# Making half of the second query tile from x * g behind the first products, and keeping two first tiles and this one in SBUF

## The chip, the cores and the metric

The kernel runs on one core of one Trainium2 chip, as one launch. The metric is device microseconds of one execution. The kernel before takes 1150.07 us, the median of three runs (1149.07 to 1150.61).

## What is computed

One layer of a decoder trunk on a sequence of 1024 tokens and 1024 channels, in float32. The part that matters here is its start: a normalised and modulated input u, and one combined projection of it.

```python
def _rmsnorm(x, g):
    y = x32 * lax.rsqrt(jnp.mean(x32 * x32, axis=-1, keepdims=True) + EPS)
    return y.astype(x.dtype) * g

u = _rmsnorm(h, g_mix) * (1 + scale1) + shift1          # scale1, shift1 from silu(c) @ W_ada + b_ada
proj = u @ w_in                                          # [q | k | v | us | gate_att | gate_ssm]
...                                                      # dilated attention, S5 branch, merge, w_out
h = h + gate1 * merged @ w_out
h = h + gate2 * ConvGatedMLP(modulate(h))
out = rmsnorm(h, g_final)
```

q, k and v have 512 columns each (8 heads of 64), us has 256, and each gate has 1024.

## The kernel before

**Precision.** Every product of two float32 matrices is made of three matmuls in a fast float32 form. Each operand is split into a high part (ScalarE, a copy) and a low part (VectorE, the value less its high part), and `mm3` (L188) adds high x high, high x low and low x high in one PSUM bank. A product of a 128-column weight tile with 512 tokens over 1024 channels is thus 8 x 3 = 24 matmuls of 128 x 512.

**Start.** Channels lie on the partitions, tokens along the free axis, and "half" 0 or 1 is the first or last 512 tokens. For each of eight channel tiles k, x is loaded (`load_x`, L330), and its 128 modulation factors g = g_mix * (1 + scale1) come from row dots of W_ada with silu(c) on VectorE (`row_dot`, L326). `xg[k]` is x * g, split in high and low. The products with weights `w0` (first 128 columns of q, first 128 of k, all 256 of us: four tiles) start from xg at once (loop at L424 to L453): x * g needs no token norm, since 1/rms is one factor for each token and can be put on afterwards, and the shift adds a constant per output column. Seven of the eight (tile, half) pairs are made there, each in its own PSUM bank, in the order of `b0` (L341): (1,0), (2,0) in banks of tag "s", (0,0), (3,0) in "t", (1,1), (2,1) in "mm", (0,1) in "o". The eighth, (3,1), is made much later from u (`gen_us`, L649). There are eight PSUM banks, two of each tag.

**The token norm.** The same x is loaded a second time with tokens on the partitions (`xn`, L352). ScalarE squares and sums each of eight tiles (L356), then `root` (L394) makes 1/rms: a table load and one activation (L397), one square (L399), two short VectorE corrections (L400, L401). `spread_a` (L405) puts it on the diagonal of four 128 x 128 blocks on ScalarE (L408), and `spread_b` (L410) multiplies by a matrix of -1 on TensorE (L413) and copies the bank to `rr` (L414). The list `late` (L416) says at which place of the product loop each of these is emitted.

**After it.** With rr known, `u_half` (L478) makes u for one channel tile and one half: VectorE (L1482), ScalarE (L1483), VectorE (L1488). `scale_r` (L466) multiplies a bank of first products by rr into `t0`, a tile in SBUF, which gives the bank back. The constant of each output column comes from a product of the weights with the shift (L494, L495: sixteen matmuls of 512 columns), transposed in `bias_cols` (L507). Then v is made for all tokens (L573 to L614): half 0 of u with banks s, s, t, t, then half 1 with mm, mm, o, o, 192 matmuls in all, while VectorE and ScalarE make the next u tiles between them; `put_q`, `put_k`, `put_v` and `put_us` write results out in split form.

**Attention.** `attention` (L1575) goes in steps of score, softmax, transpose and product with v, starting `LEAD` = 9 steps early. Between them it takes "fill" units from `gen_fill` (L659): one unit is one `mm3`. The fills make the q and k tiles of the head pairs 1 to 3 from u (`gen_qk`, L638: four groups of eight units each), the eighth us half, and then the gates and projections. Their pace is a count wanted per step: `FILL_PACE` = 1.55 units until 96 have been made, then `SLOW_PACE` = 1.52 (L1685 to L1689). Each engine runs its instructions in the written order; the pace uses a clock of its own (`unit`), not the chip's.

**Loads.** All loads of this part are issued by SyncE, in order; a weight tile uses one of two single staging buffers, "wvx" for even and "wraw" for odd numbers (`load_w`, L299).

## Time and profile before

| what | value |
|---|---|
| three timed executions | 1150.07, 1150.61, 1149.07 us |
| the profiled execution | 1151.31 us |
| its span, first to last instruction | 1149.2 us |
| mean granted TensorE clock | 0.990 of full |
| HBM read, written | 126.20 MB, 31.46 MB |

All times inside the program below are microseconds from the start of the span. The profile gives for each instruction its engine (PE is TensorE's matmul, DVE VectorE, ACT ScalarE, POOL GpSimd, SPq the load queue of SyncE), the line of the kernel, the tile written and read, and in brackets the idle time before it with the instruction that ended this wait. Matmuls overlap in the array, so the time from start to start, and not the duration shown, is what one costs in a row of them. A granted clock of 0.50 means that the array ran at half speed.

### The profile page before, as it was taken

To read this page: it belongs to the slowest core of one execution; us is meant where nothing else is said; L and a number is where in the kernel's file an instruction comes from. 1 tells how busy PE (TensorE), PEld (TensorE's weight loads), DVE (VectorE), ACT (ScalarE), POOL (GpSimd) and SP (SyncE) were. 2 spreads that over 40 slices of the span, in tenths; PEclk is the share of its full clock that TensorE was granted. 3 is DMA by queue.
4 is the path that set the end of the run, shared out by engine and by line. 5 is a ranking of instruction groups with operands and counts; after the bars stand their busy time and mean duration, and the time that the engine had idled before them with its cause. 6 is when DMAs were issued, how large, how long until landed. Compare 5 with 4: busy or idle time off the path is not lost.

```text
span 1149.2 us, 14743 instructions
## 1 busy us (share of the span) xinstructions
PE 1110.8 (97%) x5286; PEld 914.6 (80%) x5286; DVE 863.8 (75%) x1656; ACT 582.8 (51%) x1065; POOL 150.6 (13%) x171
## 2 busy tenths in 40 slices
PE   9899999999999999989899999999999999999995
PEld 8677888888878888878788887788888888877784
DVE  6678687876569598168786779888877768879876
ACT  3648777778832313243234565452445336726653
POOL 1001444445422212100000000000000000000003
PEclk9999999999999999989999999999999999999998
DMA  9811111111022221235583352245424337779433
GB/s 366 351 55 57 63 38 38 48 45 65 11 76 81 49 84 55 74 123 180 185 352 121 96 234 74 92 174 193 140 80 144 113 110 264 251 260 376 149 128 147
DMA packets 57338, 159.20 MB, mean 139 GB/s; under 512 B 7441, under 2 KB 13713, under 8 KB 55473
## 3 DMA queue, kind: packets, MB, share of 16 engines
q1 hardware_dynamic: 47520, 144.56, 35.2%
q10 hardware_dynamic: 9744, 13.70, 3.8%
q8 instruction: 41, 0.67, 0.2%
q14 instruction: 33, 0.26, 0.1%
HBM read 126.20 MB, written 31.46 MB: 137 GB/s over the span
## 4 chain that ended last, share of the span: by engine, by line
PE 63%; DVE 13%; DMA 8%; issue 8%; ACT 7%; POOL 1%; SPq 0%; POOLq 0%; ACTq 0%; DVEq 0%
PE ps_s L1335 10%; PE ps_mm L1335 8%; PE ps_mm L190 7%; PE ps_mm L192 7%; PE ps_mm L191 7%; PE ps_t L1335 7%; PE ps_s L190 3%; PE ps_s L192 3%; PE ps_s L191 3%; DMA xn<-in_xn 2%; PE ps_t L1643 2%; PE ps_s L1607 1%; PE ps_o L1660 1%; PE ps_s L1608 1%; DVE op L892 1%
## 5 line engine op out<-in xcount | busy, mean ns | idle before, releaser
L1335 PE MATMUL ps_s<-op,half 128*128 128x512 f32 x792 | 190.0, 390 | 5.2 <-ACT ps_s L1349 3.2
L1335 PEld LDWEIGHTS ps_s<-op,half 128*128 128x128 f32 x792 | 148.0, 188 | 38.7 <-ACT ps_s L1349 4.5
L190 PE MATMUL ps_mm<-u,whl 128*128 128x512 f32 x360 | 144.1, 400 | 1.6 <-DVE V L534 1.1
L192 PE MATMUL ps_mm<-u,whl 128*128 128x512 f32 x360 | 140.8, 391 | 0.0
L191 PE MATMUL ps_mm<-u,whl 128*128 128x512 f32 x360 | 140.5, 390 | 0.0
L1335 PE MATMUL ps_mm<-op,half 128*128 128x512 f32 x528 | 125.2, 389 | 0.0
L1335 PEld LDWEIGHTS ps_mm<-op,half 128*128 128x128 f32 x528 | 99.1, 188 | 20.6
L1335 PE MATMUL ps_t<-op,half 128*128 128x512 f32 x432 | 103.9, 389 | 0.7 <-ACT tp L1343 0.7
L1335 PEld LDWEIGHTS ps_t<-op,half 128*128 128x128 f32 x432 | 81.0, 188 | 17.9 <-ACT tp L1343 1.1
L121 POOL TENSOR_TENSOR whl<-wraw,whl 128x256 fp32r<-128x256 f32 (+2 forms) x52 | 63.4, 1220 | 203.1 <-ACT whl L118 203.1
L1449 POOL TENSOR_TENSOR hh<-hh,acc 128x512 f32<-128x512 f32 x3 | 4.3, 1441 | 654.3 <-ACT acc L1438 654.3
L192 PEld LDWEIGHTS ps_mm<-u,whl 128*128 128x128 f32 x360 | 67.6, 188 | 14.8
L190 PEld LDWEIGHTS ps_mm<-u,whl 128*128 128x128 f32 x360 | 67.8, 188 | 13.6 <-issue 2.2
L191 PEld LDWEIGHTS ps_mm<-u,whl 128*128 128x128 f32 x360 | 67.8, 188 | 10.4
L1648 DVE TENSOR_TENSOR PT<-ps_t,PT 128x512 fp32r<-128x512 f32 (+1 forms) x80 | 50.6, 633 | 28.2 <-ACT PT L1646 27.7
L1141 DVE TENSOR_TENSOR half<-scr,half 128x512 fp32r<-128x512 f32 x80 | 54.5, 685 | 16.2 <-ACT half L1140 15.9
L118 ACT ACTIVATE whl<-wraw 128x256 fp32r<-128x256 f32 (+2 forms) x72 | 48.7, 676 | 28.3 <-PE ps_s L192 14.6
L1619 ACT ACTIVATE S<-S,mcol 128x128 f32<-128x128 f32 (+3 forms) x64 | 49.3, 771 | 14.5 <-DVE mcol L1617 12.9
L1623 POOL TENSOR_SCALAR S<-S,mcol 128x128 f32<-128x128 f32 (+3 forms) x64 | 48.5, 761 | 50.0 <-DVE mcol L1622 29.2
L1140 ACT ACTIVATE half<-scr 128x512 fp32r<-128x512 f32 x80 | 49.0, 626 | 8.8 <-DVE scr L1122 6.7
L1141 DVE TENSOR_TENSOR half<-wraw,half 128x512 fp32r<-128x512 f32 x66 | 45.1, 686 | 8.0 <-ACT half L1140 7.9
L1646 ACT ACTIVATE PT<-ps_t 128x512 fp32r<-128x512 f32 (+1 forms) x80 | 43.7, 550 | 10.4 <-PE ps_t L1643 9.3
(516 smaller groups left out, 2430.9 us busy)
## 6 DMA issues: line engine op xcount, KB each, us to landing
wraw<-in_wup SPq DMA_DIRECT2D x32, 512.0 KB, 3.6
fq<-f SPq DMA_DIRECT2D x16, 1024.0 KB, 5.3
ft<-fq SPq DMA_DIRECT2D x14, 1024.0 KB, 7.8
ada<-in_wada SPq DMA_DIRECT2D x24, 512.0 KB, 8.8
wraw<-in_wdn SPq DMA_DIRECT2D x20, 512.0 KB, 5.7
adaB<-in_wada ACTq DMA_DIRECT2D x16, 512.0 KB, 4.3
wraw<-in_wout SPq DMA_DIRECT2D x16, 512.0 KB, 3.6
hd<-h SPq DMA_DIRECT2D x12, 512.0 KB, 7.5
```

The lines of the kernel that those rows point to most:

```text
L118: nc.scalar.activation(w[:, 0, cs], raw[:, cs], AF.Copy)
L121: lo.tensor_sub(w[:, 1, cs], raw[:, cs], w[:, 0, cs].bitcast(F32))
L190: nc.tensor.matmul(ps, wh, xh, start=first, stop=False)
L191: nc.tensor.matmul(ps, wh, xl, start=False, stop=False)
L192: nc.tensor.matmul(ps, wl, xh, start=False, stop=last)
L1140: nc.scalar.activation(w[:, 0], src, AF.Copy)
L1141: lows.append(lambda: nc.vector.tensor_sub(w[:, 1], src, w[:, 0].bitcast(F32)))
L1335: mm = lambda wp, xp, i: nc.tensor.matmul(ps, w[:, wp, ws], xp[:, cs], start=first and k + i == 0, stop=k == KT // 2 - 1 and i == 2, skip_ ...
L1619: nc.scalar.activation(tl, tl, AF.Exp, bias=mc[:, 0:1], scale=-1.0, accum_out=mc[:, 2:3])
L1623: nc.gpsimd.tensor_scalar(tl, tl, mc[:, 3:4], 0.0, op0=OP.mult, op1=OP.add)
L1646: nc.scalar.activation(pt[:, 0, :w], tps[:, :w], AF.Copy)
L1648: 0, lambda: nc.vector.tensor_sub(pt[:, 1, :w], tps[:, :w], pt[:, 0, :w].bitcast(F32)))
```

## The change

- A ninth weight tile of the start, number 8, holds the second 128 columns of q (`wq[1]`). Its load is issued in the loop at k = 4, its high part is made at k = 6 and its low part at (7, 0), ahead of `root`. It uses the staging buffer "wvx", which weight 4 (the first of v) uses after it.
- At k = 7 the first two finished banks, (1,0) and (2,0), are copied by ScalarE to their `t0` tiles in SBUF (`keep`). Their norm factor is put on later, from SBUF to SBUF.
- One of the two "s" banks so freed takes a new product, half 0 of the second q tile from xg: a loop of eight `mm3` behind the first products. `spread_b(0)` is emitted inside this loop, ahead of its seventh `mm3` (`SPREAD_AT` = 6). The product is called (3, 1) in `t0`.
- Its column constant needs sixteen matmuls of 128 columns more and a copy `brow1`, which is emitted ahead of the second `u_half`.
- `scale_r` works on (3,1) in the place of (1,0) in the first `u_half`; (1,0) and (2,0) come at k = 2 and k = 5 of the v loop.
- In attention, `gen_qk` makes only three groups for head pair 1; the finished half `q1` is written by `put_q`. The pace of the fills is 1.42 until 88 units (`FILL_QK`).

The diff, cut to its core (line numbers of the order below differ by one from the kernel before up to L413, since one line is added at the top):

```diff
+SPREAD_AT, FILL_QK = 6, 88
-LEAD, FILL_PACE, SCORE_PACE = 9, 1.55, 1.2
+LEAD, FILL_PACE, SCORE_PACE = 9, 1.42, 1.2
-            src = I["w0"][i] if i < 4 else I["wv"][i - 4]
+            src = I["wq"][1] if i == 8 else I["w0"][i] if i < 4 else I["wv"][i - 4]
+        t0, t0_pages = {}, {}
+        def tile_of(i):
+            if i[0] // 2 not in t0_pages:
+                t0_pages[i[0] // 2] = b.A([P, 4, HF], F32, "t0")
+            t0[i] = t0_pages[i[0] // 2][:, 2 * (i[0] % 2) + i[1]]
+        def keep(i, ps):
+            tile_of(i)
+            nc.scalar.activation(t0[i], ps, AF.Copy)
-        for fn, at in ((row_dot, DOTS), (root, ((7, 0),)), (spread_a, ((7, 2),))):
+        for fn, at in ((row_dot, DOTS), (root, ((7, 0),)), (spread_a, ((7, 2),)), (lambda _: wq1_low(), ((7, 0),))):
...
+            if k == 4:
+                load_w(8)
             elif k == 6:
+                wq1, wq1_low = split_hi(8)
                 for n in range(4, KT):
                     square(n)
...
                 b.mm3(ps, w[:, 0], w[:, 1], xg[k][:, 0, halves[hf]], xg[k][:, 1, halves[hf]], k == 0, k == KT - 1)
+                if k == KT - 1 and n < 2:
+                    keep((t, hf), ps)
                 b.unit(0.65)
+        b0.pop((1, 0))
+        b0.pop((2, 0))
+        b0[3, 1] = ps = b.ps("s")
+        for k in range(KT):
+            if k == SPREAD_AT:
+                spread_b(0)
+            b.mm3(ps, wq1[:, 0, k * P:(k + 1) * P], wq1[:, 1, k * P:(k + 1) * P],
+                  xg[k][:, 0, halves[0]], xg[k][:, 1, halves[0]], k == 0, k == KT - 1)
+            b.unit(0.65)
             del xg[k]
-        spread_b(0)
...
+                tile_of(i)
+                nc.vector.tensor_mul(t0[i], b0.pop(i) if i in b0 else t0[i], rr[:, halves[0 if i == (3, 1) else i[1]]])
...
+        bps1 = b.ps("s")
+        for k in range(KT):
+            ks = slice(k * P, (k + 1) * P)
+            nc.tensor.matmul(bps1[0:2, 0:P], shl[:, k], wq1[:, 0, ks], start=k == 0, stop=False)
+            nc.tensor.matmul(bps1[0:1, 0:P], shl[:, k, 0:1], wq1[:, 1, ks], start=False, stop=k == KT - 1)
-        u_half(0, 0, (1, 0))
+        u_half(0, 0, (3, 1))
+        nc.scalar.activation(brow1, bps1[0:2, 0:P], AF.Copy)
-        u_half(1, 0, (2, 0))
+        u_half(1, 0)
...
-                        u_half(k + 1, 0, *{3: [(1, 1)], 4: [(2, 1)], 5: [(0, 1)]}.get(k, []))
+                        u_half(k + 1, 0, *{2: [(1, 0)], 3: [(1, 1)], 4: [(2, 1)], 5: [(0, 1), (2, 0)]}.get(k, []))
+                        q1 = t0[3, 1]
+                        nc.scalar.activation(q1, q1, AF.Identity, bias=bias0[:, 4:5])
...
                 for hf in range(2):
+                    if (p, j, hf) == (1, 0, 0):
+                        b.spawn(put(p, hf, q1))
+                        continue
-        if want > 96:
-            want = 96 + (want - 96) / FILL_PACE * SLOW_PACE
+        if want > FILL_QK:
+            want = FILL_QK + (want - FILL_QK) / FILL_PACE * SLOW_PACE
```

How the order moves is shown at three places. First TensorE, from the last of the first products on. `ps_o_173` is the last of the seven banks, `xg_374` and `xg_376` are x * g of channel tile 7, `tp` is the diagonal of 1/rms, and `shl` is the shift. Before:

```order
L192 MATMUL ps_o_173<-xg_374,whA_335 128x512
L413 MATMUL ps_o_468<-tp_448,nones_110 128x512
L494 MATMUL ps_o_482<-whl_180,shl_474 2x512
L495 MATMUL ps_o_482<-whl_180,shl_474 1x512
L494 MATMUL ps_o_482<-whl_180,shl_474 2x512
```

Now, where `ps_s_477` is the new product with the weights `whA_405`, and the spread is L414; ahead of these rows stand five more of its `mm3`, on the five channel tiles before:

```order
L191 MATMUL ps_s_477<-xg_304,whA_405 128x512
L192 MATMUL ps_s_477<-xg_304,whA_405 128x512
L193 MATMUL ps_s_477<-xg_304,whA_405 128x512
L414 MATMUL ps_o_496<-tp_457,nones_110 128x512
L191 MATMUL ps_s_477<-xg_341,whA_405 128x512
L192 MATMUL ps_s_477<-xg_341,whA_405 128x512
L193 MATMUL ps_s_477<-xg_341,whA_405 128x512
L191 MATMUL ps_s_477<-xg_376,whA_405 128x512
L192 MATMUL ps_s_477<-xg_376,whA_405 128x512
L193 MATMUL ps_s_477<-xg_376,whA_405 128x512
L515 MATMUL ps_o_514<-whl_180,shl_506 2x512
```

Eighteen matmuls stand ahead of the spread that had none ahead of it, and six behind it, ahead of the first matmul for the column constants.

Second ScalarE, from the last four squares of x to the second u tile. Before:

```order
L356 ACTIVATE xn,ssq<-xn 128x1024 x4
L397 ACT_TABLE_LOAD
L397 ACTIVATE ssq<-ssq,epsc 128x8
L399 ACTIVATE tp<-ssq 128x8
L408 ACTIVATE tp<-ident,ssq 128x128 x4
L414 ACTIVATE rr<-ps_o 128x512
L310 ACTIVATE whA<-wvx 128x1024
L1483 ACTIVATE u<-xk,mod 128x512 x2
```

Now, where L318 is the high part of the new weights, L426 the two copies to `t0`, and L529 the copy of the new column constants:

```order
L318 ACTIVATE whA<-wvx 128x1024
L357 ACTIVATE xn,ssq<-xn 128x1024 x4
L398 ACT_TABLE_LOAD
L398 ACTIVATE ssq<-ssq,epsc 128x8
L400 ACTIVATE tp<-ssq 128x8
L426 ACTIVATE t_449<-ps_s 128x512
L426 ACTIVATE t_455<-ps_s 128x512
L409 ACTIVATE tp<-ident,ssq 128x128 x4
L415 ACTIVATE rr<-ps_o 128x512
L311 ACTIVATE whA<-wvx 128x1024
L1520 ACTIVATE u<-xk,mod 128x512
L529 ACTIVATE brow_554<-ps_s 2x128
```

The copies that free the "s" banks stand behind the four squares and the root, and the copy of the new constants stands between the first and the second u tile.

Third VectorE, around the root's corrections (`ISA ada,mod` is a row dot, with the read of its sum behind it). Before:

```order
L1504 ISA ada,mod<-ada,cpage 128x1024
L1504 ISA mod 128x1
L400 SCALAR_TENSOR_TENSOR tp<-ssq,tp 128x8
L401 SCALAR_TENSOR_TENSOR ssq<-tp,ssq 128x8
L1504 ISA ada,mod<-ada,cpage 128x1024
```

Now, where L319 is the low part of the new weights:

```order
L1541 ISA ada,mod<-ada,cpage 128x1024
L1541 ISA mod 128x1
L319 TENSOR_TENSOR whA<-wvx,whA 128x1024
L401 SCALAR_TENSOR_TENSOR tp<-ssq,tp 128x8
L402 SCALAR_TENSOR_TENSOR ssq<-tp,ssq 128x8
```

The low part stands behind the row dot of the seventh of the eight shift rows, and ahead of the root's corrections.

More of the change, by code (lines that the diff above doesn't have):

```diff
@@ L451, in body @@
                 b.mm3(ps, w[:, 0], w[:, 1], xg[k][:, 0, halves[hf]], xg[k][:, 1, halves[hf]], k == 0, k == KT - 1)
+                if k == KT - 1 and n < 2:
+                    keep((t, hf), ps)
                 b.unit(0.65)
+        b0.pop((1, 0))
[7 more added lines that the diff above has]
+            b.unit(0.65)
             del xg[k]
-        spread_b(0)
+        del ps
         b.drain()
         u = []
-        t0 = {}
-        for e in range(2):
-            page = b.A([P, 4, HF], F32, "t0")
-            for j in range(4):
-                t0[2 * e + j // 2, j % 2] = page[:, j]
-        del page
         def scale_r(*ii):
             for i in ii:
-                nc.vector.tensor_mul(t0[i], b0.pop(i), rr[:, halves[i[1]]])
+                tile_of(i)
+                nc.vector.tensor_mul(t0[i], b0.pop(i) if i in b0 else t0[i], rr[:, halves[0 if i == (3, 1) else i[1]]])
         def u_a(k, hf):
@@ L495, in body @@
             nc.tensor.matmul(bps[0:1], shl[:, k, 0:1], w[:, 1], start=False, stop=k == KT - 1)
+        bps1 = b.ps("s")
[3 more added lines that the diff above has]
+            nc.tensor.matmul(bps1[0:1, 0:P], shl[:, k, 0:1], wq1[:, 1, ks], start=False, stop=k == KT - 1)
+        wq1 = wq1_low = None
         del w
@@ L498, in body @@
         u.append(b.A([P, 2, S], R32, "u"))
-        u_half(0, 0, (1, 0))
+        u_half(0, 0, (3, 1))
         u.append(b.A([P, 2, S], R32, "u"))
-        u_half(1, 0, (2, 0))
+        brow1 = pg1.tile([2, P], F32, name="brow1")
+        nc.scalar.activation(brow1, bps1[0:2, 0:P], AF.Copy)
+        del bps1
+        u_half(1, 0)
         scale_r((0, 0), (3, 0))
@@ L504, in body @@
         nc.scalar.activation(brow[0:2], bps[0:2], AF.Copy)
-        bias0 = pg1.tile([P, 4], F32, name="bias0")
+        bias0 = pg1.tile([P, 5], F32, name="bias0")
         def bias_cols():
@@ L510, in bias_cols @@
                 nc.tensor.transpose(cps[:, 2 * t:2 * t + 2], brow[0:2, t * P:(t + 1) * P], ident[0:2, 0:2])
-            bcp = pg1.tile([P, 8], F32, name="bcp")
-            nc.scalar.activation(bcp, cps[:, 0:8], AF.Copy)
+            nc.tensor.transpose(cps[:, 8:10], brow1, ident[0:2, 0:2])
+            bcp = pg1.tile([P, 10], F32, name="bcp")
+            nc.scalar.activation(bcp, cps[:, 0:10], AF.Copy)
             nc.vector.tensor_add(bias0, bcp[:, 0::2], bcp[:, 1::2])
@@ L630, in body @@
         t0.clear()
+        t0_pages.clear()
         del us0, x
```

## The prediction

> **What bounds the kernel now.** I first read the page's busy time.
>
> ```profile
> PE 1110.8 (97%) x5286; PEld 914.6 (80%) x5286; DVE 863.8 (75%) x1656; ACT 582.8 (51%) x1065; POOL 150.6 (13%) x171
> ```
>
> TensorE is busy 97% of 1149.2 us, so the time falls only where TensorE idles or where its work shrinks. The change adds 16 small matmuls and moves 24. Next I cut the start, the v stage and attention into windows (columns: length, then busy time and count on PE, PEld, DVE, ACT and POOL, then the granted clock, the DMA share, GB/s).
>
> ```profile
> 20.00:40.00 20.00, 20.00 (x90) 16.57 (x89) 16.25 (x24) 10.84 (x13) 0.00 (x0) 1.00 1.03 419
> 50.48:53.90 3.42, 0.00 (x0) 0.00 (x0) 2.53 (x5) 2.86 (x8) 0.00 (x0) 1.00 0.69 283
> 53.90:57.31 3.41, 2.26 (x3) 0.59 (x4) 0.69 (x5) 1.25 (x4) 0.00 (x0) 0.50 0.01 4
> 57.31:60.72 3.41, 3.41 (x9) 1.00 (x8) 2.49 (x3) 1.43 (x2) 0.00 (x0) 0.50 0.10 18
> 64.35:110.13 45.78, 44.21 (x193) 35.40 (x193) 37.83 (x70) 29.48 (x68) 4.78 (x2) 1.00 0.11 35
> 110.13:320.00 209.87, 206.69 (x1222) 176.50 (x1223) 149.65 (x446) 160.35 (x350) 95.71 (x129) 1.00 0.15 49
> ```
>
> Until about 50 us the loads run full (419 GB/s). Around 52 us TensorE does nothing, and then runs at half clock up to 60.72. In the v stage and in attention it is busy nearly always: attention leaves 3.2 of 209.87 us idle. So the hole behind the first products is what new work could fill. Its edges, in TensorE's timeline (start, duration, line, tile, idle time before):
>
> ```profile
> 35.79 0.39 PE L191 MATMUL ps_s<-xg,whA 128*128 128x512 f32 x1
> 48.93 0.39 PE L192 MATMUL ps_o<-xg,whA 128*128 128x512 f32 x1
> 54.37 2.08 PE L413 MATMUL ps_o<-tp,nones 128*128 128x512 f32 x2 [5.04 <-ACT tp L408]
> 57.51 0.63 PE L495 MATMUL ps_o<-whl,shl 128*1 128x512 f32 x1
> 57.94 0.63 PE L494 MATMUL ps_o<-whl,shl 128*2 128x512 f32 x1
> 61.77 0.40 PE L495 MATMUL ps_o<-whA,shl 128*1 128x512 f32 x1
> 62.00 0.39 PE L494 MATMUL ps_o<-whA,shl 128*2 128x512 f32 x1
> 64.35 0.50 PE L190 MATMUL ps_t<-whA,u 128*128 128x512 f32 x1 [0.36 <-DVE t L468]
> 65.82 1.02 PE L413 MATMUL ps_o<-tp,nones 128*128 128x512 f32 x2
> 66.28 0.79 PE L190 MATMUL ps_s<-whA,u 128*128 128x512 f32 x1
> ```
>
> A 512-column matmul costs (48.93 - 35.79) / 58 = 0.227 us at full clock and 57.94 - 57.51 = 0.43 at half. The spread takes 2.08 us at half clock and 1.02 at full, of which TensorE is taken 0.46 (66.28 - 65.82). What fills the hole on ScalarE and VectorE:
>
> ```profile
> 49.54 1.06 ACT L356 ACTIVATE xn<-xn 128x1024 f32<-128x1024 f32 x1 [0.51 <-DMA xn<-in_xn]
> 50.70 1.28 ACT L397 ACT_TABLE_LOAD   x1
> 52.33 0.21 ACT L399 ACTIVATE tp<-ssq 128x8 f32<-128x8 f32 x1
> 53.03 1.28 ACT L408 ACTIVATE tp<-ident,ssq 128x128 f32<-128x128 f32 x4 [0.49 <-DVE ssq L401]
> 56.48 0.60 ACT L414 ACTIVATE rr<-ps_o 128x512 f32<-128x512 f32 x1 [2.17 <-PE ps_o L413]
> 50.87 1.23 DVE L1504 CUSTOM_DVE_ANT_0 ada<-ada,cpage 128x1024 f32<-128x1024 f32 x1 [2.95 <-DMA ada<-in_wada]
> 58.05 1.23 DVE L311 TENSOR_TENSOR whA<-wvx,whA 128x1024 fp32r<-128x1024 f32 x1 [3.36 <-ACT whA L310]
> 63.61 1.28 DVE L468 TENSOR_TENSOR t<-ps_t,rr 128x512 f32<-128x512 f32 x2
> ```
>
> The chain is: last x tile lands at 49.54, square, table load, root, diagonal, spread, rr at 57.08, and 7.3 us later, after u work on VectorE and ScalarE, the first "t" bank is free at about 64.3 and the v stage gets its third bank. I follow this point, "t free".
>
> **The change, part by part.**
>
> *The load of weight 8.* 512 KB are put into the full queue ahead of the last two x tiles and shift rows 4 to 7: 524 kB / 419 GB/s = 1.25 us for each of these. The last x lands at about 50.8, row 6 at 52.1. The loads of v weights 4 and 5 move behind the low part of weight 8, which frees "wvx": near 54.5. Such a load takes 3.6 us in the page's list of loads, so they are there by 58.4 and 60.
>
> ```profile
> wraw<-in_wup SPq DMA_DIRECT2D x32, 512.0 KB, 3.6
> ```
>
> That is hidden as long as rr is later than about 59. Uncovered (rr at 57.1) it costs about 1 us. In attention a k weight load now stands ahead of a bias table load on the same queue; SyncE has time there, 0.
>
> *When the new product can start.* Not at 49.3. Its bank is freed by the first copy, which stands on ScalarE behind squares and root: 52.54 (end of L399) + 1.25 + 0.6 (the copy, as L414) = 54.4. Its third matmul waits for the low part, behind the row dot on VectorE: 50.87 + 1.2 + 1.25 + 1.2 (as L311) = 54.5. Both say 54.4: the hole stays as long as it was (5.04 us), and the clock falls as it did.
>
> *The eighteen matmuls ahead of the spread.* At full clock 18 x 0.227 = 4.1 us. While the clock is halved, each microsecond does 0.53 of that. Before, it came back with the first window of 3.41 us that was wholly busy (57.31 to 60.72); 2.26 busy of 3.41 didn't suffice. Restarted at 54.4 and busy throughout, the array stays slow for 3.4 to 6.8 us; if a nearly full window will do, 2.3. I take 4.6: the eighteen end at 54.4 + 4.1 + 0.47 x 4.6 = 60.65 (59.6 to 61.7). The diagonal, ready at about 56.3 (behind both copies), waits for them. Spread 1.02, rr 0.60: rr at 62.3, 5.2 late.
>
> The Trainium skill, "TensorE: Matmul & The Clock Gate", Part 1, has the clock halved only after a whole idle window of about 3.4 us, in windows that run freely. The trace has the clock halved behind windows with work in them too:
>
> ```profile
> 487.39:490.80 3.41, 1.50 (x8) 0.93 (x6) 0.12 (x1) 2.65 (x3) 0.00 (x0) 1.00 0.00 0
> 490.80:494.21 3.41, 2.15 (x5) 1.36 (x6) 1.82 (x1) 1.07 (x2) 0.00 (x0) 0.50 0.00 0
> ```
>
> 1.50 us busy of 3.41 was little enough. However a hole of 5.04 falls, some window has at least 2.5 of it and so under 0.9 busy: I count on the fall. By the skill's rule a hole of 5.04 holds a whole window in half of the executions, and that case is a rival below.
>
> *Behind the spread.* TensorE: 60.65 + 0.46 + 6 x 0.227 = 62.5, then 16 constants by 0.23 (61.77 to 62.00) = 3.7, then the 16 new ones of 128 columns. The nearest rows:
>
> ```profile
> 113.65 0.22 PE L1607 MATMUL ps_s<-KH,QS 128*128 128x128 f32 x1
> 113.70 0.28 PE L1608 MATMUL ps_s<-KL,QS 128*128 128x128 f32 x1
> 113.82 0.33 PE L1607 MATMUL ps_s<-KH,QS 128*128 128x256 f32 x1
> 62.94 0.75 DVE L1488 SCALAR_TENSOR_TENSOR u<-xk,mod,u 128x512 fp32r<-128x512 f32 x1 [0.20 <-ACT u L1483]
> 79.51 0.16 ACT L512 ACTIVATE bcp<-ps_o 128x8 f32<-128x8 f32 x1
> 62.81 0.57 ACT L504 ACTIVATE tp<-ps_o 2x512 f32<-2x512 f32 x1
> 97.79 1.93 ACT L519 ACTIVATE t<-t,bias 128x512 f32<-128x512 f32 x3
> ```
>
> 0.05 to 0.12 each; 0.09 makes 1.4 and an end at 67.6. The new copy (between 0.16 and 0.57; 0.3) waits for it on ScalarE, and behind it stand u's second ScalarE step (0.65, by L519's three in 1.93), VectorE's L1488 (0.7) and one scaling (1.28 / 2): t free at 69.9, 5.6 late. By rr alone, with one scaling of 0.65 fewer, it would be 4.5 late. The clock's ends move it by 1.05 either way, the dearer copy and matmuls by 0.8 more: 4.6 to 7.4.
>
> *The v stage.* One scaling more on VectorE falls under waits for ScalarE at k = 2, half so at k = 5 (0.5); one more pass over 128x512 on ScalarE (0.6) lies in the chain that ends the stage, ahead of the last v copies. TensorE waited on that chain already:
>
> ```profile
> 103.76 0.50 PE L192 MATMUL ps_mm<-whA,u 128*128 128x512 f32 x1 [0.48 <-DVE u L1488]
> 110.13 0.47 PE L190 MATMUL ps_mm<-u,whl 128*128 128x512 f32 x1 [1.09 <-DVE V L534]
> ```
>
> So + 1.1 (0 to 1.3), and attention starts 6.7 us late (4.6 to 8.7).
>
> *Attention.* 24 matmuls go: 24 x 0.227 = 5.4 us, and 5.8 if the small gaps beside them go too. Per step the pace drops by 0.13 units, so the steps come faster; ScalarE (160.35 of 209.87) and VectorE (149.65) have room for 2.6%. Lower bound 3.5, if a third returns as waits. I take 5.4.
>
> Sum: + 6.7 - 5.4 = + 1.3 us (4.6 - 5.8 = -1.2 to 8.7 - 3.5 = + 5.2). On the profiled execution (1151.31, of which 1149.2 is span) that is 1152.6; it lies 1.2 above the median, so against the median 1150.07 it is **1151.4**. About 0.2% (2.3 us) is what a measurement of this kernel tells from no change: this is none.
>
> **Rivals.**
>
> - *The hole is filled (faster).* If the copies and the low part came before the root, the eighteen would run 49.4 to 53.5, the diagonal end at 55.6, rr at 57.2, TensorE's constants at 62.6, t free at 64.9 (0.6 late), attention 1.7 late: - 3.7, 1146.4. For it: both banks are complete by 46 us. Against: the order of ScalarE and VectorE, which run as written. Chance 0.13; this is also the case that the change does what it seems to do.
> - *Attention doesn't give it back (slower).* If the shorter steps are set by ScalarE's and VectorE's chain (score, minimum, exponential, transpose), 24 matmuls fewer save about 2 us: + 4.7, 1154.8. It decides from the point where less than 4.4 of the 5.4 comes back. For it: ScalarE is 76% busy, and the late start moves extra writes of q to the first steps. Against: TensorE's idle time there is 3.2 us of 210. Chance 0.20.
> - *The clock doesn't fall.* The eighteen end at 58.5, rr at 60.1, t free at 67.8 (3.5 late), attention 4.6 late: - 0.8, 1149.3. Chance 0.12, since the trace shows the fall in such a hole. (The Trainium skill's rule above would make it half.)
>
> **How the numbers follow.** My forecast has 0.55, the rest as above. Of its own range most lies within 0.2% (0.38), 0.14 above, 0.03 below. Faster 0.13 + 0.03 + 0.01 = 0.17, same 0.38 + 0.11 = 0.49, slower 0.14 + 0.20 = 0.34. The range leaves out most of the first rival and the far end of the second: 1148.0 to 1155.0. The likeliest case alone spans 1149 to 1154.
>
> **What would show it.** Right: in the profile after, TensorE idle for about 5 us from 49.3, ended by the copy or the low part; clock 0.50 behind it; rr near 62; attention starting near 117; attention 5 us shorter. Wrong: new matmuls at 50 us; rr before 59; or an attention stage shorter by under 4 or over 6.5 us.

## The result and the profile after

The changed kernel takes 1155.4 us (median of four runs, 1153.05 to 1156.07), the kernel before, beside it, 1149.71. The ratio is 1.0052, with a 95% interval of 1.0037 to 1.0067: slower by 0.5%, clear of the interval's 0.15% to either side, and 0.4 us above my range. A second set of runs of the same kernel (below) gave 1155.59 and 1.0051.

The profiled execution took 1154.92 us, 1153.1 of it span. On the page, TensorE is busy 0.8 us less than before and the span is 3.9 longer, so what is new is waiting:

```profile
PE 1110.0 (96%) x5303; PEld 916.3 (79%) x5303; DVE 867.4 (75%) x1658; ACT 584.4 (51%) x1070; POOL 150.7 (13%) x171
```

**The start went nearly as I had written it.** TensorE's timeline of the changed kernel, from the end of the first products to attention's first matmul and first long wait:

```profile
53.99 0.65 PE L191 MATMUL ps_s<-xg,whA 128*128 128x512 f32 x1 [5.08 <-ACT t L426]
...
59.83 1.02 PE L414 MATMUL ps_o<-tp,nones 128*128 128x512 f32 x2
...
65.83 0.22 PE L521 MATMUL ps_s<-whA,shl 128*1 128x128 f32 x1
...
66.68 0.23 PE L521 MATMUL ps_s<-whA,shl 128*1 128x128 f32 x1
...
69.26 0.50 PE L191 MATMUL ps_t<-whA,u 128*128 128x512 f32 x1 [0.93 <-DVE t L489]
...
116.13 0.47 PE L191 MATMUL ps_mm<-u,whl 128*128 128x512 f32 x1 [1.26 <-DVE V L565]
...
123.13 0.44 PE L1644 MATMUL ps_s<-KH,QS 128*128 128x384 f32 x1 [2.17 <-DVE mcol L1647]
```

The hole is 5.08 us and ends with ScalarE's copy; the eighteen matmuls end at 59.83; the first "t" bank is used at 69.26 instead of 64.35, 4.9 late; attention starts 6.0 late. The clock falls behind the hole and is back after one wholly busy window (columns as in the prediction; the third number from the end is the granted clock):

```profile
50.77:54.18 3.41, 0.19 (x1) 0.19 (x2) 2.48 (x5) 3.35 (x7) 0.00 (x0) 1.00 0.09 36
54.18:57.59 3.41, 3.41 (x9) 2.64 (x9) 1.79 (x6) 1.51 (x5) 0.00 (x0) 0.50 0.70 220
57.59:61.01 3.42, 3.42 (x15) 2.46 (x14) 0.00 (x0) 0.13 (x1) 0.00 (x0) 1.00 0.22 90
```

**Attention did not give it back.** The stretch that I call attention below goes from its first matmul (a fill unit) to the sixteenth transpose of `W1T`, a tile of the S5 branch. That is 60 us behind attention's own last transpose in the kernel before and in the changed one (58 in e12). Before and after:

```profile
110.13:380.86 270.73, 266.40 (x1526) 225.30 (x1527) 191.47 (x561) 179.23 (x379) 110.97 (x139) 1.00 0.17 54
```

```profile
116.13:384.39 268.26, 260.55 (x1502) 220.59 (x1503) 193.22 (x561) 178.43 (x379) 111.16 (x139) 1.00 0.17 54
```

24 matmuls fewer, and TensorE is busy 266.40 - 260.55 = 5.85 us less, a little more than the 5.4 I had counted. But it idles 268.26 - 260.55 = 7.71 instead of 4.33. So attention is only 2.5 us shorter, and its end 3.5 us late. (Up to attention's own last transpose it takes 210.38 us before and 207.77 after: 2.6 less.) Which waits are new stands in the list of TensorE's waits there, before and then after (columns: what waits, for whom, us in total, times, longest):

```profile
PE ps_s L1607 <- DVE mcol L1610: 1.2, 4, 0.4
...
PE ps_t L1643 <- DVE mcol L1622: 0.3, 1, 0.3
```

```profile
PE ps_s L1644 <- DVE mcol L1647: 3.8, 4, 2.2
PE ps_t L1680 <- DVE mcol L1659: 1.3, 3, 0.7
```

Scores wait for score minima (L1647), transposes for the factors of the softmax (L1659). The longest of these, 2.17 us, is at attention's start. There VectorE first finishes the write of the new tile into QS, and only then makes the first minimum:

```profile
121.34 0.69 DVE L577 SCALAR_TENSOR_TENSOR QS<-t,QS 64x512 fp32r<-64x512 f32 x1 [2.98 <-ACT QS L574]
122.06 0.69 DVE L580 SCALAR_TENSOR_TENSOR QS<-t,QS 64x512 fp32r<-64x512 f32 x1
122.78 0.29 DVE L1647 CUSTOM_DVE_ANT_0 S<-ps_s,near 128x128 f32<-128x128 f32 x1
```

In the kernel before, the product for this write was still to come, and the first minimum stood at the head, where it waited for its bias table:

```profile
114.88 0.29 DVE L1610 CUSTOM_DVE_ANT_0 S<-ps_s,near 128x128 f32<-128x128 f32 x1 [2.52 <-DMA near<-in_bt]
```

That is 4.75 us after attention's start; now it is 6.65 us. Both "s" banks are full, and TensorE stands. The second group of waits is at 162 to 170.

Times are best read by stage, since the rest behind attention differs by 2.3 us between two executions of the changed kernel alone, and from 765.9 to 768.7 in these seven. Worked out from the traces (start of attention's first matmul, of the last of those transposes, their difference, and from there to the last instruction's end):

| execution profiled | attention starts | attention ends | attention | the rest |
|---|---|---|---|---|
| before | 110.13 | 380.86 | 270.73 | 768.4 |
| changed | 116.13 | 384.39 | 268.26 | 768.7 |
| changed, again (e5) | 117.64 | 387.57 | 269.93 | 766.4 |
| write later (e1) | 117.00 | 383.85 | 266.85 | 765.9 |
| hole filled (e2) | 114.49 | 384.44 | 269.95 | 766.2 |
| start mended (e10) | 112.33 | 379.05 | 266.72 | 766.1 |
| control (c3) | 108.09 | 378.74 | 270.65 | 767.4 |

So the profiled executions of before and after both had a long rest. Of the two of the changed kernel one is 3.5 us late at the end of attention and the other 6.7; the medians are 5.4 to 5.7 apart. The difference between the two is explained under theory C.

### The profile page after: what moved, and what is told of

It is laid out like the page before. It is cut to its first block, busy times and chain, and to the rows that moved or that the text cites. A ratio compares the mean times of both kernels' runs of the same rounds, so it can differ in the third digit from the quotient of the medians.

```text
span 1153.1 us, 14787 instructions
## 1 busy us (share of the span) xinstructions
PE 1110.0 (96%) x5303; PEld 916.3 (79%) x5303; DVE 867.4 (75%) x1658; ACT 584.4 (51%) x1070; POOL 150.7 (13%) x171
## 4 chain that ended last, share of the span: by engine, by line
PE 69%; DVE 12%; ACT 8%; DMA 6%; issue 3%; POOL 1%; SPq 0%; ACTq 0%; POOLq 0%; DVEq 0%
PE ps_s L1372 13%; PE ps_mm L1372 9%; PE ps_t L1372 8%; PE ps_mm L191 7%; PE ps_mm L193 7%; PE ps_mm L192 7%; PE ps_s L191 3%; PE ps_s L192 3%; PE ps_s L193 3%; DMA ada<-in_wada 2%; PE ps_t L1680 2%; DMA xn<-in_xn 2%; ACT S L1656 1%; PE ps_s L1644 1%; PE ps_s L1645 1%
## 5 line engine op out<-in xcount | busy, mean ns | idle before, releaser
L191 PE MATMUL ps_mm<-u,whl 128*128 128x512 f32 x352 | 141.1, 401 | 1.8 <-DVE V L565 1.3
L193 PE MATMUL ps_mm<-u,whl 128*128 128x512 f32 x352 | 137.7, 391 | 0.0
L192 PE MATMUL ps_mm<-u,whl 128*128 128x512 f32 x352 | 137.5, 391 | 0.0
L193 PEld LDWEIGHTS ps_mm<-u,whl 128*128 128x128 f32 x352 | 66.1, 188 | 14.4
L191 PEld LDWEIGHTS ps_mm<-u,whl 128*128 128x128 f32 x352 | 66.3, 188 | 13.4 <-issue 2.4
L192 PEld LDWEIGHTS ps_mm<-u,whl 128*128 128x128 f32 x352 | 66.4, 189 | 10.0
L1178 DVE TENSOR_TENSOR half<-scr,half 128x512 fp32r<-128x512 f32 x80 | 54.5, 684 | 16.2 <-ACT half L1177 16.1
L1680 PEld LDWEIGHTS ps_t<-ident,S 128*128 128x128 f32 x288 | 35.5, 140 | 15.5 <-issue 4.6
```

The costliest lines, as they stand in the source:

```text
L191: nc.tensor.matmul(ps, wh, xh, start=first, stop=False)
L192: nc.tensor.matmul(ps, wh, xl, start=False, stop=False)
L193: nc.tensor.matmul(ps, wl, xh, start=False, stop=last)
L1178: lows.append(lambda: nc.vector.tensor_sub(w[:, 1], src, w[:, 0].bitcast(F32)))
L1680: nc.tensor.transpose(tps[:, n * P:(n + 1) * P], sl[:, o:o + P], ident)
```

## The experiments

Theory A: the write of the new tile at attention's head causes the wait of 2.17 us. Theory B, the rival from the prediction: the chain of score, minimum, exponential and transpose has no room for shorter steps, wherever the write stands. Two more came up on the way. C: that wait lets the clock fall in some executions. D: a copy of K on VectorE stands still beside GpSimd and causes the waits at 162 to 170.

### The write of the new tile (A)

```diff
-                        b.spawn(put(p, hf, q1))
+                        b.spawn(put(p, hf, q1), Q1_AT)
```

`Q1_AT` is 4.0 us of the program's own planning clock, which sets where in the order the write comes.

> The changed kernel with the write of the new tile into QS put behind the first three exponentials instead of ahead of the first score minimum (two ScalarE and two VectorE instructions moved; nothing else). Theory A (the write at the head fills both score banks and costs TensorE the wait of 2.17 us at 123.13): that wait is gone, the first minimum starts near 120.5 instead of 122.78, and the time is 1.5 to 2.2 us under that of the changed kernel, about 1153.5, or 1.003 of the kernel before. Theory B (the shorter steps are set by the chain of score, minimum, exponential and transpose, wherever the write stands): the wait comes back at other places of the first 10 us and the time stays at 1155.4 within 0.7.

Measured: 1152.07 us, ratio to the kernel before 1.0021 (1.0012 to 1.0031). The wait is gone, and the first minimum waits for its bias table, as before:

```profile
121.47 0.29 DVE L1647 CUSTOM_DVE_ANT_0 S<-ps_s,near 128x128 f32<-128x128 f32 x1 [2.24 <-DMA near<-in_bt]
```

The longest wait in the first 13 us is now 0.48. Attention lasts 266.85 us, 3.9 less than before. A holds against B for this wait. The gain is more than A said: 3.5 us in the medians, not 2. What is still missing lies later: 40 to 60 us behind attention's start TensorE idles 2.09 us in this trace and 0.49 in the kernel before.

### The clock (C)

In the run that filled the hole (below) the same wait, 2.20 us there, was followed by a window at half clock. So the changed kernel was run again as it is.

> The changed kernel as it is, beside the next three on one chip, for its spread. Theory C (the wait of 2.17 us at the first score minima sometimes lets the clock fall to one half for a window of 3.41 us, which costs about 1.6 us more, as in the trace of the run with the hole filled): its executions lie between 1152 and 1156.5, in two groups some 1.5 us apart, median near 1153.5 to 1155.5. If the wait never costs clock: one group near 1153.3 (the kernel before plus the 3.5 us that the profile shows at the end of attention).

Measured: 1155.59 us (1155.2 to 1155.76), ratio 1.0051 (1.0036 to 1.0066). One group, but at the upper place. Its trace has the wait (2.23 us) within one window:

```profile
121.70:125.11 3.41, 1.19 (x6) 0.72 (x5) 2.01 (x6) 3.35 (x5) 0.00 (x0) 1.00 0.66 254
125.11:128.52 3.41, 3.41 (x10) 2.71 (x9) 0.70 (x4) 1.42 (x6) 0.83 (x2) 0.50 0.01 2
```

In the first trace of the changed kernel the wait fell across two windows, and neither was empty enough:

```profile
119.03:122.45 3.42, 1.93 (x11) 1.34 (x9) 1.08 (x2) 2.95 (x5) 0.00 (x0) 1.00 0.96 364
122.45:125.86 3.41, 2.73 (x12) 2.33 (x13) 1.89 (x10) 2.51 (x7) 0.83 (x2) 1.00 0.06 24
```

Attention lasted 269.93 us there against 268.26: 1.7 us more, half a window. C holds for these two traces and for the one below (e2). Four traces have the write at the head: the clock fell in two, behind windows busy for 1.19 (e5) and 1.21 us (e2), and not in the two others, busy for 1.93 (the first) and 1.63 (e6, below). How often it falls in the executions that were only timed is a guess from their times. The start too took one window more at half clock in e5 than the first time: the window in which the new product began was busy for only 2.27 us, and attention started 1.5 us later:

```profile
53.43:56.84 3.41, 2.27 (x5) 1.83 (x6) 3.09 (x10) 2.80 (x9) 0.00 (x0) 0.50 0.32 73
56.84:60.26 3.42, 3.42 (x9) 2.65 (x8) 0.00 (x0) 0.00 (x0) 0.00 (x0) 0.50 0.59 236
```

### The hole and the load

```diff
-(root, ((7, 0),)), (spread_a, ((7, 2),)), (lambda _: wq1_low(), ((7, 0),))
+(root, ((7, 2),)), (spread_a, ((7, 3),)), (lambda _: wq1_low(), ((6, 5),)), (lambda a: square(6 + a), ((7, 2), (7, 2)))
-                for n in range(4, KT):
+                for n in range(4, 6):
                     square(n)
```

> The changed kernel with ScalarE's two copies ahead of the last two squares and the root, and the low part of weight 8 ahead of VectorE's row dot of row 6. If the order on ScalarE and VectorE alone kept the hole: the copies end at about 49.7, the low part at 50.2, TensorE is idle for about 1.5 us instead of 5.08, no window at clock 0.5 near 57, rr at 57.5 to 58.5 instead of 61.48, attention starts 1.5 to 2.5 us late instead of 6.0. Theory A (the write of the new tile into QS costs its own 2.2 us in attention): net 1.1 to 1.8 below the kernel before, 1148.3. Theory B (attention gives back 2.6 whatever its start is): the same within 0.6, so this run does not tell A from B. If something else held the product back (the bank, the load), the hole stays above 4 us and the time at 1155.

Measured: 1152.92 us, 1.0023 (1.0013 to 1.0034). The order on ScalarE and VectorE did keep the hole. But rr came at 58.93, and attention started 4.4 late, not 2. TensorE waited 2.04 us for the diagonal behind the eighteen matmuls, that window fell to 1.37 us busy, and the clock fell once more, as it did behind the write at attention's head:

```profile
53.50:56.91 3.41, 1.37 (x6) 0.80 (x5) 1.60 (x7) 2.45 (x7) 0.00 (x0) 1.00 0.42 167
56.91:60.32 3.41, 3.41 (x8) 2.11 (x7) 0.41 (x1) 1.54 (x2) 0.00 (x0) 0.50 0.00 0
...
118.35:121.76 3.41, 1.21 (x6) 0.74 (x6) 1.99 (x6) 3.35 (x5) 0.00 (x0) 1.00 0.78 296
121.76:125.18 3.42, 3.42 (x10) 2.75 (x10) 0.73 (x6) 1.57 (x6) 0.83 (x2) 0.50 0.01 4
```

From the fifth score on it runs within 0.1 us of the times of the first trace of the changed kernel: 1.6 us earlier at attention's start, 1.6 lost there to the clock.

The load of weight 8 alone, put into the kernel before (with its split, and no product):

```diff
+            if k == 4:
+                load_w(8)
...
+                wq1, wq1_low = split_hi(8)
```

> The kernel before with only the load of weight 8 and its split into a high and a low part added, at the changed kernel's places; the new product isn't made. It prices the load alone. As forecast: the last x tile lands 1.25 us later, rr is about 1 us later (58.1), the time 1.0 us more, 1150.7. If the low part on VectorE delays the root's two VectorE steps as well: up to 2.2 us more. If the delay is taken up by waits behind it: no change within 0.4.

Measured: 1151.15 us, 1.0009 (0.9999 to 1.0019). The last square starts 1.06 us later, the low part on VectorE delays the root's steps further, and the spread comes 1.6 us later behind a longer hole:

```profile
56.00 2.08 PE L413 MATMUL ps_o<-tp,nones 128*128 128x512 f32 x2 [6.66 <-ACT tp L408]
```

rr is at 58.71, attention starts 1.8 late. The load and split alone cost 1.3 us by the medians (1.0 expected), though the interval just takes in no change. In the changed kernel this delay should be part of the time at which the copies, behind the squares, end the hole; no run takes it out alone.

### Attention alone, and the pace

The kernel before without the 24 matmuls (a part of the computation is left out), with the new pace:

```diff
+                    if (p, j, hf) == (1, 0, 0):
+                        continue
...
+                    if (p, j) == (1, 0):
+                        b.spawn(put(p, 0, ps), 1.3)
```

> The kernel before with the 24 matmuls of the second query tile's first half left out of attention, nothing put in front, the pace 1.42 and 88 as in the changed kernel; both halves of that tile are written from the second half's bank (this leaves out part of the computation, so the output is not the reference's). It prices what attention gives back when neither the start is late nor the write stands at its head. Theory A: 5.0 to 5.8 us less than the kernel before, 1144.3, TensorE's idle time in attention stays near 3 us. Theory B (chain of score, minimum, exponential, transpose sets the shorter steps): 2 to 3 us less, 1147.1, and TensorE's idle time there rises to 5.5 us or more.

Measured: 1147.45 us, 0.998 (0.997 to 0.9991), attention 268.32. That is the number of theory B (A had 1144.3), and TensorE idles 7.49 us, as B said. But the waits have other reasons: the two writes from one bank stand together on VectorE and make a wait of their own, 1.37 us, and the rest are the waits of the changed kernel at 162 to 170. With the 1.37 added, the 2.4 us that attention gave here come to 3.8, as in e1. So this run does not price attention without a write ahead of a minimum, as it was meant to.

```profile
123.93 0.44 PE L1611 MATMUL ps_s<-KH,QS 128*128 128x384 f32 x1 [1.37 <-DVE mcol L1614]
```

If the shorter steps were the trouble, the old pace should help. The kernel of the first experiment with it:

```diff
-LEAD, FILL_PACE, SCORE_PACE = 9, 1.42, 1.2
+LEAD, FILL_PACE, SCORE_PACE = 9, 1.55, 1.2
```

> The kernel of the first experiment with the fill pace of the first steps back at 1.55 (three matmuls of fill in 1.55 of a step, as before), so that the first 57 steps are as long as in the kernel before and the matmuls saved come off behind them. Theory B (shorter steps leave ScalarE, VectorE and GpSimd no room): the waits at 160 to 170 shrink to those of before (under 0.8 us in sum), and attention gives back 1 to 2 us more than the 3.9 there, time 1150.5 to 1151. Theory D (only where a copy happens to fall): another chance placement, anything from 1150 to 1153, and single copies of 1.8 us or more beside GpSimd would show it.

Measured: 1155.51 us, 1.0051 (1.0036 to 1.0066), and attention 270.57, as long as before: all that the 24 matmuls gave is lost. The waits grew, and TensorE idles 9.47 us in attention instead of 5.98; one wait at 165.13 is 2.05 us. B fails in this form: the shorter steps are not the trouble, and of the two paces only 1.42 has the gain. Why the waits grew is not shown.

### The waits at 162 to 170 (D)

VectorE and GpSimd in the changed kernel:

```profile
145.27 0.42 DVE L592 CAST KH<-KH 64x512 fp32r<-64x512 f32 x1
...
158.93 2.52 DVE L592 CAST KH<-KH 64x512 fp32r<-64x512 f32 x1
...
162.21 0.16 DVE L1654 TENSOR_TENSOR mcol<-mcol 128x1 f32<-128x1 f32 x1
```

```profile
158.76 0.73 POOL L1712 TENSOR_TENSOR Oat<-tp,Oat 64x256 fp32r<-64x256 f32 x1 [3.29 <-ACT Oat L1711]
159.47 1.01 POOL L1660 TENSOR_SCALAR S<-S,mcol 128x896 f32<-128x896 f32 x1
160.44 0.72 POOL L122 TENSOR_TENSOR whl<-wraw,whl 128x256 fp32r<-128x256 f32 x1
```

```profile
162.23 0.39 PE L1644 MATMUL ps_s<-KH,QS 128*128 128x256 f32 x1 [1.02 <-DVE mcol L1647]
167.25 0.52 PE L1680 MATMUL ps_t<-ident,S 128*128 128x128 f32 x3 [0.66 <-DVE mcol L1659]
169.81 0.63 PE L1680 MATMUL ps_t<-ident,S 128*128 128x128 f32 x4 [0.40 <-DVE mcol L1659]
```

The copy of K from one half of the partitions to the other takes 2.52 us; the one at 145.27 takes 0.42. It starts 0.2 us after the first of three GpSimd instructions in a row, and ends 0.3 after the last of them. The minimum behind it, and TensorE's score, wait. The Trainium skill, "SBUF — State Buffer", section "SBUF: two separate sides", has VectorE and GpSimd share one pair of ports under an exclusive lock, held for a whole instruction. These rows agree; if the lock is the cause, three of GpSimd's instructions in a row kept VectorE from it for 2.1 us (2.52 less 0.42).

First cure, the copies on ScalarE, with the write at the head (e6) and later (e7):

```diff
-            nc.vector.tensor_copy(kh[64:128, 0, hs], kh[0:64, 0, hs].bitcast(F32))
+            copy_k(p, kh[64:128, 0, hs], kh[0:64, 0, hs])    # nc.scalar.activation for p > 0
```

> The changed kernel with VectorE's copies of K between the two partition halves put on ScalarE for the last three pairs of heads (12 copies; the write of the new tile stays at the head). Theory D (one such copy, 2.52 us at 158.93 instead of 0.42, stands still beside three instructions of GpSimd, and TensorE's waits of 1.02, 0.66 and 0.40 us at 162 to 170 come from it): these waits are gone, the end of attention is 1.5 to 2.1 us earlier, the time about 2 us under the changed kernel's. Theory B (the shorter steps are set by the chain of score, minimum, exponential, transpose): waits of the same sum come back within the next 15 us, the time as the changed kernel's within 0.7.

> The changed kernel with both: the write of the new tile behind the first three exponentials, and the copies of K on ScalarE. Theories A and D together: attention takes the whole 5.0 to 5.8 us less than before, the end of attention lies 0.5 to 1.5 us later than in the kernel before, time 1150.3 to 1151.3 against 1149.8, that is within 0.2% of the kernel before (the sum as I had forecast it). Theory B: attention gives back 2.6 to 3.9 and the time stays at 1152 or more.

Measured: 1159.31 us, 1.008 (1.0064 to 1.0095), and 1156.27, 1.0062 (1.0044 to 1.008): about 4 us slower than without. With twelve activations more, ScalarE is late with its copies of transposes, VectorE waits for them and TensorE for VectorE, 2.20 us at 167.71 (VectorE's row in e6):

```profile
166.87 0.69 DVE L1686 TENSOR_TENSOR PT<-ps_t,PT 128x512 fp32r<-128x512 f32 x1 [3.09 <-ACT PT L1684]
```

And VectorE's next instruction stands still in the copy's place, a minimum of 128 x 1 numbers that takes 0.16 us in the changed kernel (at 162.21, above). It ends with the last of GpSimd's three:

```profile
160.52 1.67 DVE L1655 TENSOR_TENSOR mcol<-mcol 128x1 f32<-128x1 f32 x1
```

Second cure, the copies read from PSUM, with the write later:

```diff
+            nc.vector.tensor_copy(kh[64:128, 0, hs], ps[0:64] if p else kh[0:64, 0, hs].bitcast(F32))
```

> The kernel of the first experiment (write of the new tile later) with VectorE's copies of K between the halves of partitions read from the score product's PSUM bank instead of from SBUF (12 copies for the last three pairs of heads). Theory D (the copy of SBUF to SBUF stands still beside GpSimd): a copy takes about 0.7 us everywhere, also at 158, TensorE's waits of 1.04, 0.66 and 0.39 us go, the time is 1.5 to 2.1 us under that run's 1152.1, about 1150.3. Theory B (around the change of pair ScalarE, VectorE and GpSimd together have no room for shorter steps, and whichever instruction comes next stands still): the waits return in another row, as with the copies on ScalarE, and the time stays at 1152 within 0.7.

Measured: 1170.33 us, 1.0189 (1.0172 to 1.0206). The copies take 0.68 or 0.69 us each, as D said, and the scores' and transposes' waits shrink to 0.3 us each. But the copies now hold the product's bank, and the fills wait 14 us for it (TensorE's waits, as above), so the run does not show what the shorter copies alone are worth:

```profile
PE ps_mm L191 <- DVE KH L594: 14.0, 6, 3.3
```

Third, the copies as they are, only moved in VectorE's order for the second pair of heads, ahead of and behind GpSimd's three instructions. Both start from the kernel with the start mended (next part), which has the wait too (1.03 us).

```diff
-            yield 0.7
+            yield K_AT[0] if p == 1 else 0.7        # e13: 0.3 and 0.0; e14: 2.0 and 0.7
```

> The kernel with the start mended; VectorE's copies of K for the second pair of heads stand one step earlier, where GpSimd is idle (from 150.2 to 153.5). Theory D: both copies take 0.42, the wait of 1.03 us at 157 is gone and most of the 0.66 and 0.40 behind it, end of attention 1.0 to 1.8 us earlier (377.6), time 1145.4 against 1146.8. Theory B (whatever VectorE does next with two inputs in SBUF stands still beside GpSimd instead): the same waits in another row, time 1146.8 within 0.5.

> The same with these copies one step later, behind GpSimd's three instructions. Theory D: as above, unless the first scores of the second pair, which need the copies, then wait for them (up to 1 us). Theory B: time 1146.8 within 0.5.

Measured: 1147.24 us, 0.9982 (0.9972 to 0.9991), and 1146.87, 0.9977 (0.9966 to 0.9988), against 1146.78 and 0.998 without the move: no change. In e13 the copies take 0.42 each, and the minimum takes their place beside GpSimd (1.38 us in e14):

```profile
154.85 1.47 DVE L1656 TENSOR_TENSOR mcol<-mcol 128x1 f32<-128x1 f32 x1
```

TensorE still waits 1.28 us, now at 161.20. The end of attention comes 0.7 and 0.5 us earlier. So D fits the long instructions, but there is no single guilty one: at this place VectorE had one with its inputs in SBUF beside GpSimd in each order tried. That the missing 1.5 us come from there alone is not shown, since GpSimd's own order wasn't changed.

### The change with its start mended

Everything at once, with the copies of K on ScalarE (e8), then on VectorE as they were (e10): the hole filled as above, the write later, the spread behind all 24 new matmuls, the copy of the new constants behind the second u tile:

```diff
-SPREAD_AT, FILL_QK = 6, 88
+SPREAD_AT, FILL_QK, Q1_AT = 8, 88, 4.0
...
-        nc.scalar.activation(brow1, bps1[0:2, 0:P], AF.Copy)
         u_half(1, 0)
+        nc.scalar.activation(brow1, bps1[0:2, 0:P], AF.Copy)
```

> All of these and the hole filled: copies of the two first tiles ahead of the last two squares, the low part of weight 8 ahead of row 6, all 24 matmuls of the new product ahead of the spread, the copy of the new constants behind u's second ScalarE step, the write of the new tile later, the copies of K on ScalarE. By the sum: rr near 58.9, t free near 66.2 (1.9 late), attention starts 2 to 3 us late and takes 5.4 less: 2.4 to 3.4 us under the kernel before, about 1146.8, ratio 0.9975. Theory B: attention gives back 2.6 and the time equals the kernel before within 1 us.

> The kernel with everything changed, but the copies of K back on VectorE as they were: hole filled, 24 matmuls ahead of the spread, copy of the new constants later, write of the new tile later. The start as there: rr near 58.6, attention starts 2.5 us late; attention gives back what it gave with the write later (3.9): 1.4 us under the kernel before, about 1148.6, ratio 0.9988. If the copies of K on ScalarE weren't what cost 4.8 us in that run: 1151.5 as there.

Measured: e8 1151.55 us, 1.0011 (1.0001 to 1.0021), not the 1146.8 expected: the price of ScalarE's copies once more, as e10 shows. e10 1146.78 us, 0.998 (0.997 to 0.9989): 2.5 us under the kernel before, where 1.4 was expected. The traces show 1.8 of it at the end of attention. No window near the start falls to half clock. TensorE still waits a little at each joint:

```profile
56.45 1.13 PE L414 MATMUL ps_o<-tp,nones 128*128 128x512 f32 x2 [0.79 <-ACT tp L409]
...
58.27 0.40 PE L517 MATMUL ps_o<-whl,shl 128*2 128x512 f32 x1 [0.69 <-ACT rr L415]
...
65.48 0.50 PE L191 MATMUL ps_t<-whA,u 128*128 128x512 f32 x1 [0.27 <-DVE t L491]
```

rr is at 58.22, t free 65.48 (1.1 late), attention 2.2 late, and gives back 4.0.

### The order of loads, in both kernels

The 1.1 us that rr is still late I put down to the load. Shift rows 0 to 5 were put behind the x tiles in the load queue, first with only the low part of weight 8 further ahead on VectorE (e11), then with the row dots of rows 6 and 7 behind the root on VectorE (e15), then with the spread behind 15 matmuls (e16). The kernel before with the same loads and dots is the control (c3, and c4 beside e16).

```diff
-            if 3 <= k < 7:
-                load_row(2 * k - 6)
-                load_row(2 * k - 5)
             if 2 <= k < 6:
...
+            if 3 <= k < 7:
+                load_row(2 * k - 6)
+                load_row(2 * k - 5)
```

> The same with the shift rows 0 to 5 behind the x tiles and weight 8 in the load queue, and the low part of weight 8 further ahead on VectorE: the last x lands 2 x 1.25 = 2.5 us earlier, the new product follows the first ones without a hole (under 1 us), rr at 56 to 57, t free near 63.5, attention starts within 0.8 us of the kernel before: 3 to 4.5 us under the kernel before, about 1146.1, ratio 0.9967. If the shift rows, now later, hold up the constants: t free at 65 or later, time about 1147.6.

Measured: 1147.49 us, 0.9986 (0.9973 to 0.9998). The last square ended 1.9 us earlier, and rr came at 58.31 all the same: the root's two steps stood behind the row dots on VectorE, and the diagonal waited 1.95 us for them.

> The kernel with the loads reordered, and in it the row dots of rows 6 and 7 behind the two steps of the root on VectorE (there the last square was done at 50.7, 1.9 us earlier than without, but the root's VectorE steps came at 54.23 behind these dots). rr at 55.5 to 56.3 instead of 58.3, attention starts 2.0 to 2.6 us earlier than there, time about 1144.6, ratio to the kernel before 0.9955. If the constants (shift rows) now hold u up: rr earlier, but attention's start by less than 1 us.

> Control: the kernel before with the same order of loads (shift rows behind the x tiles) and of row dots, nothing else. If the last x was what set rr: it lands 2.5 us earlier, rr at 54.6 to 55.2 instead of 57.08, attention starts 1.9 to 2.5 us earlier, time about 1147.3, ratio 0.998. If the shift rows hold up the constants: less than 1 us.

Measured: e15 1147.77 us, 0.998 (0.9971 to 0.999), with rr at 58.20 again: TensorE was now busy without a gap up to the spread, and ScalarE waited for it. So with the spread behind all 24 matmuls an earlier load brought nothing.

```profile
57.61 0.60 ACT L415 ACTIVATE rr<-ps_o 128x512 f32<-128x512 f32 x1 [3.23 <-PE ps_o L414]
```

The control took 1146.29 us, 0.9973 (0.9961 to 0.9985). Its spread waits 1.87 us where the kernel before waited 5.04:

```profile
52.12 1.35 PE L413 MATMUL ps_o<-tp,nones 128*128 128x512 f32 x2 [1.87 <-ACT tp L408]
```

rr is at 54.11, and attention starts 2.0 us earlier than before.

> The kernel with loads and row dots reordered and everything else mended, the spread now behind 15 of the 24 new matmuls. The diagonal is ready at 54.4 there: the spread starts at 54.4 to 54.8 instead of 56.55, rr at 56.0 instead of 58.2, attention starts 1.5 to 2.2 us earlier (110.1 to 110.8), time about 1145.2 against 1147.8 (and against 1146.3 of the control: 1 us under it). If the matmuls of the constants, then behind 9 more of the new ones, set u: rr earlier, attention's start by less than 1 us, time as the control's.

> The control (the kernel before with loads and row dots reordered) once more, beside the last one: 1146.3 within 0.7, ratio 0.9973.

Measured: e16 1147.27 us, 0.9979 (0.9969 to 0.9988), with rr at 56.43 and attention at 110.63 about as expected, but not the time (1145.2); c4 1148.01 us, 0.9984 (0.9974 to 0.9993). In the traces attention ends at 377.53 in e16, at 378.74 in c3 and at 379.64 in c4, so the mended change is 1 to 2 us ahead there. The medians (0.74 us apart on one chip, intervals overlapping) don't settle whether anything of that reaches the end.

## Why the prediction was wrong

- **The hole stays, the clock falls: right.** 5.08 us against 5.04, ended by the copy at 53.99 (forecast 54.4).
- **Eighteen matmuls, spread, rr: right, a little dear.** They end at 59.83 (forecast 60.65) and rr is at 61.48 (62.3), because the clock came back after one window. In e5 it took two, the eighteen ended at 61.44 and rr was at 63.09. Both ends lie in the bounds given (59.6 to 61.7).
- **The loads: one sum slips.** 54.5 + 3.6 is 58.1, not 58.4, for v weight 4; nothing else rests on it.
- **Small matmuls and copy: right.** (66.68 - 65.83) / 14 = 0.06 us each (0.09), and 0.27 (0.3).
- **t free and attention's start: right.** 4.9 and 6.0 late in the first trace, 6.5 and 7.5 in the second (forecast 5.6 and 6.7, bounds 4.6 to 7.4 and 4.6 to 8.7).
- **Attention gives back 5.4, at least 3.5: this step failed.** It gave back 2.5 us in the first trace and 0.8 in the second. TensorE's work fell by more than 5.4, so the count of matmuls was sound; waits had been put at nothing in the sum, and the allowance in the lower bound, "if a third returns", was too small. The parts: 2.2 us of waiting behind the write at the head, 1.4 of it net (268.26 - 266.85); 1.7 more where that wait emptied a window and the clock fell; and 1.5 that is missing from 5.4 even with the write later (3.9 to 4.0 came back). In e1's trace this lies at 157 to 177, where TensorE idles 1.6 us more than in the same stretch of the kernel before; its cause is shown only in part (theory D).
- **The reason I gave against the second rival was the error.** TensorE's 3.2 us of idle time in 210 showed that it had not waited with that order. It said nothing of an order in which the first minimum stands 1.9 us further behind attention's start. I had named the writes among the reasons for that rival, and not priced them: two on ScalarE and two on VectorE, 0.6 to 0.7 us each, ahead of an instruction for which both score banks wait. That rival's time, 1154.8, came nearest to the measured one, but only its writes are shown as a cause (e1). Its chain, as something that sets every step, is not: one place kept waiting (162 to 170), and the old pace did not help (e12).
- **The first rival** (hole filled, 1146.4) was worth less than written: 4.4 late at attention's start, not 1.7, with only the copies and the low part moved. It took the later spread, the later copy of the constants and the later write as well to reach 1146.8.

## What to carry to other kernels

Work taken off the bound engine was worth its time here only where nothing else was put ahead of the instruction that frees its banks. So price the writes that come with moved work in the queue of each engine, at the place where the bound engine has two banks and no more. And before a hole is filled, see what sets it: here an order of loads and row dots shortened it in the kernel before as well, for the same gain (0.9973 and 0.9984, against 0.998 for the mended change) and with less work. No run shows a gain of the change itself over that control in the time.

## What the runs showed of the hardware that I had not expected

- A wait of 2.2 us can cost 1.7 more, by where it falls. Windows busy for 1.19, 1.21 and 1.37 us of 3.41 were followed by half clock, as 1.50 was before; 1.63 and 1.93 were not. All 20 traces, divided into windows of 3.41 us in step with the clock's changes, say the same: at full clock, every window busy for 1.50 us or less was followed by half clock, and none busy for more than 1.75. Half clock ended behind windows busy for 2.72 us or more (e3 and e4) and lasted behind 2.65 or less (c3). The Trainium skill, "TensorE: Matmul & The Clock Gate", Part 1, asks for a whole idle window; these traces differ from it.
- Beside GpSimd an instruction of VectorE on 128 x 1 numbers took 1.38, 1.47 and 1.67 us (e14, e13, e6) instead of 0.16, and a copy 2.52 instead of 0.42.
